# A two-block model kernel: products ordered by part, a token tile's last products by column halves, norm rows scaled on ScalarE

## Chip, core and metric

The kernel runs on one core of one Trainium2 chip. The metric is the device time of one execution in microseconds (us). TensorE (PE) does the matrix products, VectorE (DVE), ScalarE (ACT) and GpSimd (POOL) the work on elements, and SyncE (SP) issues most transfers.

## What is computed

The input is `x`, 256 tokens of 1024 values, all in float32. Two blocks follow each other. Cut to what matters here:

```
for layer in range(2):                                  # block 1
    qkv = rms_norm(x, g_mix[layer]) @ w_in[layer]
    mix = concat(differential(qkv), moba(qkv), dilated(qkv))
    x   = x + mix @ w_out[layer]                        # 1024 x 1024
    h2  = rms_norm(x, g_ffn[layer])
    x   = x + conv_gated_mlp(h2, w_up, conv_w, conv_b, w_down)
x = rms_norm(x, g_final)
h = rms_norm(x, norm1_g)                                # block 2
x = x + gates(ssm(h), sparse_attention(h)) @ w_out_2
h = rms_norm(x, norm2_g)
x = x + peer(h)      # top-16 routing, then gelu(h @ u.T) weighted @ v, 16384 experts
return rms_norm(x)

def rms_norm(x, g): return x * rsqrt(mean(x * x) + 1e-6) * g
```

## The kernel before

**Products.** Each float32 product is made of three products of reduced-precision parts: high by high, low by high, high by low, summed in the same PSUM bank. `mm3` (lines 149 to 153) issues the three for one slice of the contraction: line 151 is high by high, lines 152 and 153 each hold one low part. Which of the two low parts is that of the weights depends on the side on which the weights enter: in the trace's rows the moving operand stands first, then the stationary one.

**Weights.** `Weights` (L64) streams weight tiles of 128x1024 through SBUF in the order in which they are used. SP issues the load into one of four `raw` buffers; ACT copies it to the high part `whi` (L92); DVE subtracts to make the low part `wlo` (L94), or POOL does, for the tiles that `share` gives it. The parts have six buffers each, three in the last stage. `take`/`next` hand out tiles and split those that come after; `more(n)` splits until n tiles past the used ones are ready; `post` and `flush` hold back the evacuation of a PSUM bank to a chosen place in the order. All engines' orders are fixed when the program is built, by the order of these calls.

**The stages.** The matrix products of each stage follow each other on PE without a break in the program: the input projections, the attentions with their small products between weight tiles, the output projection, the up- and down-projections of the gated MLP (`layer_ffn`, with `up_mm` making 24 products of 256 columns for one weight tile), block 2's projections, the routing's queries and scores, 128 tiles of `u` (`u_pair`, L1691, two tiles of 24 products of 256 columns), and 128 tiles of `v` (`v_mm`, L1785, 12 products of 512 columns).

**The seam at a norm.** An output projection ends in `token_tiles` (L606): its last four weight tiles are all split by then, and are used for token tile 0 (the first 128 tokens), both column halves per weight tile, and then for token tile 1, in an order of (weight tile, half) steps of three products. `residual` (L657) adds a finished half to `x` on DVE. `rest` calls what the next norm has armed as `after_residual`. Three of the norms are armed by `arm_norm` (L665): that ahead of the gated MLP in each layer, and that ahead of the routing. There `after` multiplies by the gain on POOL (L675), squares and sums on ACT (L181), and, once a token tile's two halves are summed, finds the root on DVE (`rstd` L188, `rsqrt` L155: a first guess from the bits and three Newton steps on 128x1 values, lines 165 and 170) and scales the two halves of the row tile on DVE (L680). `ready` then calls `norm_T` (L197): eight transposes on PE (L204), the high part on ACT (L208), the low part on DVE (L209). `norm_at` says ahead of which step of token tile 1 token tile 0's transposes stand; `pool_splits` and `head_share` say which weight tiles POOL splits there. `head` (L637) makes the products with the next projection's first four weight tiles, token tile 0 first; ahead of its fourth weight tile stand the transposes of token tile 1. `arm_roots` (L693) and `arm_double` (L1885) are the other two kinds of norm; they scale later.

## Time and profile before

| | us |
|---|---|
| median of 3 runs | 1763.09 |
| the runs | 1757.03, 1763.09, 1763.2 |
| the profiled execution | 1756.17 |
| its span | 1754.2 |

The profile is of one execution of its own; its span is the time from the first to the last recorded instruction, and the 2 us between span and time lie around it. The granted clock of TensorE is 0.983 of full speed on average over the span. A stretch at "1.00" runs at 2.4 GHz, one at "0.50" at 1.2 GHz.

### The profile page before, as it was taken

The numbers are of one execution on the slowest core, as the hardware profiler recorded it, in microseconds if no ns is written. First come the engines' busy times: TensorE is split into PE (matmuls) and PEld (weight loads), VectorE is DVE, ScalarE is ACT, GpSimd is POOL, SyncE is SP. The second block draws the span as 40 slices with busy tenths as digits, with TensorE's granted clock in tenths as the row PEclk, the third lists the DMA queues.
The fourth block names the chain that finished last, engine by engine and source line by source line (L and its number), as shares of the span: only waits on it lengthen the run. The fifth ranks groups of instructions, "written<-read, shape, count | busy, mean of one in ns | idle before, by whom it ended". The sixth has DMA issues, their size and how long they took to land.

```text
span 1754.2 us, 29812 instructions
## 1 busy us (share of the span) xinstructions
PE 1675.0 (95%) x11558; PEld 1472.5 (84%) x11558; DVE 1262.0 (72%) x2260; ACT 842.2 (48%) x1286; POOL 603.0 (34%) x534
## 2 busy tenths in 40 slices
PE   8997999899979999989989989999999999999998
PEld 6786888787869898767869989999999888887776
DVE  6776898767767776696753998667777889864444
ACT  6554554655535555643434535543343444444444
POOL 3203438432038843681020444100000232345554
PEclk9998999999989999989999999999999999999999
DMA  7433455653334567723435445554454555555554
GB/s 253 143 120 121 144 176 168 216 186 132 121 132 158 170 200 251 285 84 104 156 123 180 156 164 186 181 173 165 157 164 162 167 170 169 168 180 191 187 187 155
DMA packets 84717, 294.09 MB, mean 168 GB/s; under 512 B 10800, under 2 KB 14928, under 8 KB 83680
## 3 DMA queue, kind: packets, MB, share of 16 engines
q1 hardware_dynamic: 83184, 286.19, 49.7%
q0 software_dynamic: 960, 5.47, 0.8%
q8 instruction: 91, 1.49, 0.3%
q10 hardware_dynamic: 432, 0.53, 0.1%
q14 instruction: 50, 0.41, 0.1%
HBM read 284.42 MB, written 7.34 MB: 166 GB/s over the span
## 4 chain that ended last, share of the span: by engine, by line
PE 74%; DVE 12%; POOL 5%; ACT 3%; issue 3%; DMA 2%; POOLq 0%; ACTq 0%; DVEq 0%; SPq 0%
PE acc L151 14%; PE acc L152 13%; PE acc L153 13%; PE side L151 8%; PE side L152 8%; PE side L153 8%; DVE wlo L94 3%; PE side L1686 3%; DVE cv L760 2%; ACT whi L92 2%; DVE rs_t L165 1%; POOL th L768 1%; PE side L385 1%; DVE rs_y L170 1%; PE side L204 1%
## 5 line engine op out<-in xcount | busy, mean ns | idle before, releaser
L94 DVE TENSOR_TENSOR wlo<-raw,whi 128x1024 fp32r<-128x1024 f32 x472 | 619.4, 1322 | 327.8 <-ACT whi L92 325.1
L92 ACT ACTIVATE whi<-raw 128x1024 fp32r<-128x1024 f32 x511 | 532.7, 1056 | 501.2 <-PE acc L152 231.2
L152 PE MATMUL side<-hTh,wlo 128*128 128x256 f32 x1664 | 471.4, 283 | 16.2 <-DVE wlo L94 14.8
L151 PE MATMUL side<-hTh,whi 128*128 128x256 f32 x1664 | 472.3, 284 | 0.2
L153 PE MATMUL side<-hTl,whi 128*128 128x256 f32 x1664 | 469.7, 282 | 0.0
L152 PEld LDWEIGHTS side<-hTh,wlo 128*128 128x128 f32 x1664 | 317.6, 191 | 20.5 <-DVE wlo L94 17.7
L151 PEld LDWEIGHTS side<-hTh,whi 128*128 128x128 f32 x1664 | 317.6, 191 | 2.6 <-ACT whi L92 0.7
L153 PEld LDWEIGHTS side<-hTl,whi 128*128 128x128 f32 x1664 | 317.8, 191 | 0.0
L1774 POOL TENSOR_TENSOR al<-S,ah 128x256 fp32r<-128x256 f32 x125 | 154.1, 1233 | 465.2 <-ACT ah L1773 465.2
L152 PE MATMUL acc<-whi,al 128*128 128x512 f32 x496 | 196.4, 396 | 0.0
L151 PE MATMUL acc<-whi,ah 128*128 128x512 f32 x496 | 195.1, 393 | 0.0
L153 PE MATMUL acc<-wlo,ah 128*128 128x512 f32 x496 | 193.2, 390 | 0.0
L151 PE MATMUL acc<-whi,hTh 128*128 128x512 f32 x384 | 161.7, 421 | 1.3 <-ACT whi L92 1.3
L152 PE MATMUL acc<-whi,hTl 128*128 128x512 f32 x384 | 154.9, 403 | 0.3 <-DVE hTl L209 0.3
L153 PE MATMUL acc<-wlo,hTh 128*128 128x512 f32 x384 | 154.6, 403 | 0.1
L94 POOL TENSOR_TENSOR wlo<-raw,whi 128x1024 fp32r<-128x1024 f32 x39 | 94.8, 2435 | 132.0 <-ACT whi L92 125.2
L152 PEld LDWEIGHTS acc<-whi,al 128*128 128x128 f32 x496 | 93.1, 188 | 28.7 <-POOL al L1774 7.5
L768 POOL TENSOR_TENSOR th<-th,cv 128x256 f32<-128x256 f32 x44 | 58.3, 1328 | 158.2 <-DVE th L767 121.0
L151 PEld LDWEIGHTS acc<-whi,ah 128*128 128x128 f32 x496 | 93.1, 188 | 19.5
L153 PEld LDWEIGHTS acc<-wlo,ah 128*128 128x128 f32 x496 | 93.2, 188 | 17.8
L760 DVE SCALAR_TENSOR_TENSOR cv<-side,cw,cv 128x254 f32<-128x254 f32 (+1 forms) x176 | 72.6, 474 | 30.9 <-ACT cv L757 30.9
L151 PEld LDWEIGHTS acc<-whi,hTh 128*128 128x128 f32 x384 | 74.8, 195 | 23.5 <-issue 6.5
(460 smaller groups left out, 2583.1 us busy)
## 6 DMA issues: line engine op xcount, KB each, us to landing
raw<-in_ws SPq DMA_DIRECT2D x259, 512.0 KB, 3.6
raw<-in_us SPq DMA_DIRECT2D x128, 512.0 KB, 3.4
raw<-in_vs SPq DMA_DIRECT2D x128, 512.0 KB, 3.3
dBst<-Bst SPq DMA_DIRECT2D x1, 2048.0 KB, 7.3
dCT<-CT SPq DMA_DIRECT2D x2, 1024.0 KB, 8.4
tg<-dBst POOLq DMA_DIRECT2D x1, 2048.0 KB, 10.3
gb<-in_g_ffn SPq DMA_DIRECT2D x2, 512.0 KB, 4.6
s5bc<-in_s5bc SPq DMA_DIRECT2D x2, 512.0 KB, 5.3
```

Of the source, the lines that this page charges most:

```text
L92: self.nc.scalar.activation(hi, t, AF.Copy)
L94: eng.tensor_tensor(lo, t, hi.bitcast(FT), op=OP.subtract)
L151: mm(ps, sh, mh, start=first, stop=False)
L152: mm(ps, sl, mh, start=False, stop=False)
L153: mm(ps, sh, ml, start=False, stop=last)
L165: V.scalar_tensor_tensor(t, y, h, y, op0=OP.mult, op1=OP.mult)
L170: V.scalar_tensor_tensor(o, t, 1.5, y, op0=OP.add, op1=OP.mult)
L204: nc.tensor.transpose(ps[:, 128 * i:128 * i + 128], src[:, c:c + 128], self.ident)
L760: nc.vector.scalar_tensor_tensor(o[which][:, n:], p[which][:, :S - n], cw[which][:, 2 - n:3 - n], o[which][:, n:], op0=OP.mult, op1=OP.add)
L768: nc.gpsimd.tensor_tensor(th, th, o[1], op=OP.mult)
L1686: nc.tensor.matmul(o, e2[:, n], e1[:, n, x], start=x == 0, stop=x == 2)
L1774: G.tensor_tensor(al, src, ah.bitcast(FT), op=OP.subtract)
```

## The change

Four things are edited. **(1)** `mm3` takes a list of products and issues all their high-by-high parts first, then all of one low side, then all of the other; `late` says which side's low part comes last ("s" the stationary one, "m" the moving one). With `mm_cols` a weight tile of an up-projection, of `u` or of the queries is eight products by `whi` with the high part, eight by `whi` with the low part, eight by `wlo`. **(2)** `rsqrt` of one column uses TENSOR_SCALAR with pointer scalars in place of SCALAR_TENSOR_TENSOR. **(3)** `token_tiles` does token tile 0's last two weight tiles by column halves, so that half 0 is finished one step of three products sooner. **(4)** `arm_norm` scales rows on ACT, in `ready`, right ahead of the transposes; these stand one step later; POOL splits other tiles and `hold` makes the splits there start later.

```diff
-    def mm3(self, ps, sh, sl, mh, ml, first, last):
+    def mm3(self, todo, late):
         mm = self.nc.tensor.matmul
-        mm(ps, sh, mh, start=first, stop=False)
-        mm(ps, sl, mh, start=False, stop=False)
-        mm(ps, sh, ml, start=False, stop=last)
+        for ps, sh, sl, mh, ml, first, last in todo:
+            mm(ps, sh, mh, start=first, stop=False)
+        for side in "ms" if late == "s" else "sm":
+            for ps, sh, sl, mh, ml, first, last in todo:
+                mm(ps, sl if side == "s" else sh, ml if side == "m" else mh, start=False, stop=last and side == late)
+
+    def mm_cols(self, ps, wt, T, n=128):
+        cs = [(k, slice(128 * k, 128 * k + n)) for k in range(8)]
+        self.mm3([(ps, wt[0][:, c], wt[1][:, c], T[0][:, k], T[1][:, k], k == 0, k == 7) for k, c in cs], "s")
...
             if n == 1:
-                V.scalar_tensor_tensor(t, y, h, y, op0=OP.mult, op1=OP.mult)
+                V.tensor_scalar(t, y, y, h, op0=OP.mult, op1=OP.mult)
+                V.tensor_scalar(o, t, 1.5, y, op0=OP.add, op1=OP.mult)
...
         wts = w.take(4, 2)
-        for i in range(4):
-            if i:
+        for i, h in ((0, 0), (0, 1), (1, 0), (1, 1), (2, 0), (3, 0), (2, 1), (3, 1)):
+            if i and not h:
                 w.flush()
-            mms(0, i, wts[i], (0, 1))
-            if hook:
+            mms(0, i, wts[i], (h,))
+            if h and hook:
                 hook(i)
-        for h in range(2):
-            self.residual(0, h, ps[0][h])
-            self.rest(0, h)
+            if (i, h) == (3, 0):
+                self.residual(0, 0, ps[0][0])
+                self.rest(0, 0)
+        self.residual(0, 1, ps[0][1])
+        self.rest(0, 1)
...
-                w.more(min(3 + i, 4))
+                w.more(min(3 + max(i - self.hold, 0), 4))
...
             if h:
-                r = self.rstd(ms[:, t])
-                for x in (xn[t][:, 512 * i:512 * i + 512] for i in range(2)):
-                    self.nc.vector.tensor_scalar(x, x, r, None, op0=OP.mult)
+                root[t] = self.rstd(ms[:, t])
 
         def ready(t):
-            self.norm_T(xn.pop(t), hT, t)
+            x = xn.pop(t)
+            for h in range(2):
+                v = x[:, 512 * h:512 * h + 512]
+                self.nc.scalar.activation(v, v, AF.Identity, scale=root[t])
+            self.norm_T(x, hT, t)
 
-        self.norm_at, self.residual_at, self.pool_splits, self.head_share = (2, 1), (3, 0), (0, 1), 1
+        self.norm_at, self.residual_at, self.pool_splits, self.head_share = (3, 1), (3, 0), (0, 3), 1
+        self.hold = 2
...
         def up_mm(ps, which, wt):
-            for k in range(8):
-                c = slice(128 * k, 128 * k + 128)
-                self.mm3(ps[:, 256 * which:256 * which + 256], wt[0][:, c], wt[1][:, c], hh[:, k], hl[:, k], k == 0, k == 7)
+            self.mm_cols(ps[:, 256 * which:256 * which + 256], wt, hT)
...
-        def v_mm(c, A, wt, t, h):
-            tk = slice(128 * t, 128 * t + 128)
-            cc = slice(512 * h, 512 * h + 512)
-            self.mm3(acc[t][h], A[0][:, tk], A[1][:, tk], wt[0][:, cc], wt[1][:, cc], c == 0, c == 127)
+        def v_mm(c, A, wt, th):
+            self.mm3([(acc[t][h], *(x[:, 128 * t:128 * t + 128] for x in A), *(x[:, 512 * h:512 * h + 512] for x in wt),
+                       c == 0, c == 127) for t, h in th], "s")
```

The other callers of `mm3` get lists in the same way, with "m" (the moving weights' low part last) in the input and output projections and "s" in `head`. `arm_roots` and `arm_double` set `hold = 0`.

ScalarE at the first `arm_norm` norm, that ahead of the gated MLP of layer 0, from the attention's last evacuations (`mixTh`) to the high parts of the second token tile (`hTh`; `ms` takes the sum of squares, `rs_y` is the root), before:

```order
L448 ACTIVATE mixTh<-side 128x256 x4
L181 ACTIVATE squares,ms<-x 128x512 x2
L92 ACTIVATE whi<-raw 128x1024 x2
L208 ACTIVATE hTh<-side 128x4x128 x2
L181 ACTIVATE squares,ms<-x 128x512 x2
L92 ACTIVATE whi<-raw 128x1024 x2
L208 ACTIVATE hTh<-side 128x4x128 x2
L92 ACTIVATE whi<-raw 128x1024 x3
```

and of the change:

```order
L459 ACTIVATE mixTh<-side 128x256 x4
L192 ACTIVATE squares,ms<-x 128x512 x2
L92 ACTIVATE whi<-raw 128x1024
L192 ACTIVATE squares,ms<-x 128x512
L699 ACTIVATE xn<-xn,rs_y 128x512 x2
L219 ACTIVATE hTh<-side 128x4x128 x2
L92 ACTIVATE whi<-raw 128x1024
L192 ACTIVATE squares,ms<-x 128x512
L92 ACTIVATE whi<-raw 128x1024 x2
L699 ACTIVATE xn<-xn,rs_y 128x512 x2
L219 ACTIVATE hTh<-side 128x4x128 x2
L92 ACTIVATE whi<-raw 128x1024 x3
```

The squares of token tile 1's first half come ahead of the first `hTh`, two row scalings stand ahead of each `hTh` pair, and the two weight copies that stood between the first squares and the first `hTh` are spread out. On DVE the two scalings L680 are gone at each place, and the root's six steps stand at the same place in another form.

GpSimd at the same norm (`gb` is the gain, `xn` the row tile, `th` belongs to the gated MLP after it), before:

```order
L675 TENSOR_TENSOR xn<-x,gb 128x512 x2
L94 TENSOR_TENSOR wlo<-raw,whi 128x1024 x2
L768 TENSOR_TENSOR th<-th,cv_1686 128x256
L768 TENSOR_TENSOR th<-th,cv_1696 128x256
L768 TENSOR_TENSOR th<-th,cv_1745 128x256
```

and of the change:

```order
L690 TENSOR_TENSOR xn<-x,gb 128x512
L94 TENSOR_TENSOR wlo<-raw,whi 128x1024
L690 TENSOR_TENSOR xn<-x,gb 128x512
L94 TENSOR_TENSOR wlo<-raw,whi 128x1024 x2
L784 TENSOR_TENSOR th<-th,cv_1686 128x256
L784 TENSOR_TENSOR th<-th,cv_1696 128x256
L784 TENSOR_TENSOR th<-th,cv_1745 128x256
```

The two splits of each pair are drawn apart: one stands between the row tile's halves of token tile 1, and two after them.

PE at the end of the layer-0 `head` and the first weight tiles of the up-projection (`side` is the bank of an up-projection, `hTh` and `hTl` the two parts of the normed rows), before, where the three products of each slice alternate:

```order
L151 MATMUL acc<-whi,hTh 128x512
L152 MATMUL acc<-whi,hTl 128x512
L153 MATMUL acc<-wlo,hTh 128x512
L151 MATMUL side<-hTh,whi 128x256
L152 MATMUL side<-hTh,wlo 128x256
L153 MATMUL side<-hTl,whi 128x256
L151 MATMUL side<-hTh,whi 128x256
```

and of the change:

```order
L154 MATMUL acc<-whi,hTh 128x512 x2
L157 MATMUL acc<-wlo,hTh 128x512 x2
L157 MATMUL acc<-whi,hTl 128x512 x2
L154 MATMUL side<-hTh,whi 128x256 x8
L157 MATMUL side<-hTl,whi 128x256 x8
L157 MATMUL side<-hTh,wlo 128x256 x8
```

The first product with `wlo` of a weight tile was its second of 24, and is now its seventeenth; the last product with `whi` was its 24th, and is now its sixteenth.

## Rows read from the trace of the kernel before

**Rows 1.** The page: the span, and the busy time of each engine.

```profile
span 1754.2 us, 29812 instructions
...
PE 1675.0 (95%) x11558; PEld 1472.5 (84%) x11558; DVE 1262.0 (72%) x2260; ACT 842.2 (48%) x1286; POOL 603.0 (34%) x534
```

**Rows 2.** Waits of PE: us in total, times, longest wait in us.

```profile
PE side L204 <- DVE xn L680: 23.7, 5, 5.7
PE side L152 <- DVE wlo L94: 14.8, 13, 1.8
...
PE acc L152 <- DVE wlo L94: 4.8, 1, 4.8
```

**Rows 3.** Timeline of PE in two stages: start, length, what it does.

```profile
999.78 0.28 PE L153 MATMUL side<-hTl,whi 128*128 128x256 f32 x1
999.90 0.28 PE L151 MATMUL side<-hTh,whi 128*128 128x256 f32 x1
...
1499.71 0.39 PE L153 MATMUL acc<-wlo,ah 128*128 128x512 f32 x1
1499.94 0.39 PE L151 MATMUL acc<-whi,ah 128*128 128x512 f32 x1
```

**Rows 4.** Timeline around the first gated-MLP norm of layer 0.

```profile
130.83 1.39 DVE L659 TENSOR_TENSOR x<-acc,x 128x512 f32<-128x512 f32 x2 [2.54 <-PE acc L153]
...
131.10 0.40 PE L153 MATMUL acc<-wlo,mixTh 128*128 128x512 f32 x1
...
131.60 2.57 POOL L675 TENSOR_TENSOR xn<-x,gb 128x512 f32<-128x512 f32 x2 [17.48 <-DVE x L659]
...
133.35 0.21 DVE L191 TENSOR_SCALAR var<-ms 128x1 f32<-128x1 f32 x1 [1.13 <-ACT squares L181]
...
133.60 0.15 DVE L161 TENSOR_SCALAR rs_y<-var 128x1 int32<-128x1 int32 x1
...
134.54 4.67 POOL L94 TENSOR_TENSOR wlo<-raw,whi 128x1024 fp32r<-128x1024 f32 x2 [0.37 <-ACT whi L92]
...
134.67 2.25 DVE L170 SCALAR_TENSOR_TENSOR rs_y<-rs_t,rs_y 128x1 f32<-128x1 f32 x1
...
139.87 0.88 DVE L680 TENSOR_SCALAR xn<-xn,rs_y 128x512 f32<-128x512 f32 x2 [0.46 <-DVE rs_y L170]
...
140.51 1.94 PE L204 MATMUL side<-ident,xn 128*128 128x128 f32 x8 [4.81 <-DVE xn L680]
...
141.63 0.60 ACT L208 ACTIVATE hTh<-side 128x512 fp32r<-128x512 f32 x1 [5.77 <-PE side L204]
```

**Rows 5.** Windows: stretch, length, PE, PEld, DVE, ACT, POOL busy, granted clock.

```profile
137.80:144.60 6.80, 4.09 (x14) 3.64 (x15) 4.45 (x7) 1.80 (x4) 2.69 (x2) 0.50 0.44 155
...
sum 34.20, PE 23.74 PEld 20.65 DVE 20.16 ACT 8.23 POOL 9.40; mean PE 4.75 PEld 4.13 DVE 4.03 ACT 1.65 POOL 1.88
```

**Rows 6.** Groups of ScalarE by line and form: count, busy, mean ns.

```profile
L92 ACT ACTIVATE whi<-raw 128x1024 fp32r<-128x1024 f32 x511 | 532.7, 1056 | 501.2 <-PE acc L152 231.2 <-PE side L153 221.8 <-PE acc L153 22.0
...
L181 ACT ACTIVATE squares<-x 128x512 f32<-128x512 f32 x28 | 17.6, 630 | 30.7 <-DVE x L659 28.8 <-POOL x L1914 1.1 <-ACT squares L181 0.3
...
L1829 ACT ACTIVATE hTh<-raw,rs_y 128x512 f32<-128x512 f32 x2 | 1.4, 723 | 3.9 <-DVE rs_y L170 3.9
```

**Rows 7.** Windows: the up-projections of layer 0, and the routing.

```profile
192.00:275.00 83.00, 76.69 (x525) 69.47 (x524) 73.21 (x179) 45.66 (x69) 35.51 (x30) 1.00 0.51 165
1000.00:1032.00 32.00, 25.44 (x206) 24.62 (x204) 31.96 (x118) 11.89 (x14) 16.68 (x7) 1.00 0.37 132
```

**Rows 8.** Timeline at 221 us: GpSimd and VectorE at once.

```profile
221.13 2.39 POOL L94 TENSOR_TENSOR wlo<-raw,whi 128x1024 fp32r<-128x1024 f32 x1
...
221.24 2.32 DVE L841 TENSOR_SCALAR ex_n<-ex_n 128x16 f32<-128x16 f32 x1
```

**Rows 9.** Timeline at 1005 us, in the routing: the same pair.

```profile
1005.55 2.38 POOL L94 TENSOR_TENSOR wlo<-raw,whi 128x1024 fp32r<-128x1024 f32 x1 [2.11 <-ACT whi L92]
...
1005.77 3.25 DVE L94 TENSOR_TENSOR wlo<-raw,whi 128x1024 fp32r<-128x1024 f32 x1
```

More of the change, by code (lines that the diff above doesn't have):

```diff
@@ L168, in rsqrt @@
                 V.tensor_tensor(t, t, h, op=OP.mult)
-            o = y if out is None or i < iters - 1 else out
-            V.scalar_tensor_tensor(o, t, 1.5, y, op0=OP.add, op1=OP.mult)
+                V.scalar_tensor_tensor(o, t, 1.5, y, op0=OP.add, op1=OP.mult)
         return o
@@ L593, in mms @@
             tk = slice(128 * t, 128 * t + 128)
-            for h in hs:
-                c = slice(512 * h, 512 * h + 512)
-                self.mm3(ps[t][h], T[0][:, k, tk], T[1][:, k, tk], wt[0][:, c], wt[1][:, c], first, last)
+            cs = [(h, slice(512 * h, 512 * h + 512)) for h in hs]
+            self.mm3([(ps[t][h], T[0][:, k, tk], T[1][:, k, tk], wt[0][:, c], wt[1][:, c], first, last) for h, c in cs], "m")
         for i, k in enumerate(ks[:4]):
@@ L668, in arm_norm @@
         hT = self.new_T(self.hTp, "hT")
-        xn = {}
+        xn, root = {}, {}
         ms = self.xnp.tile([128, 2, 2], FT, name="ms")
@@ L1334, in wide @@
             tk = slice(128 * t, 128 * t + 128)
-            for h in hs:
-                c = slice(512 * h, 512 * h + 512)
-                self.mm3(ps[t][h], T[0][:, k, tk], T[1][:, k, tk], wt[0][:, c], wt[1][:, c], first, last)
+            cs = [(h, slice(512 * h, 512 * h + 512)) for h in hs]
+            self.mm3([(ps[t][h], T[0][:, k, tk], T[1][:, k, tk], wt[0][:, c], wt[1][:, c], first, last) for h, c in cs], "m")
         def ev_attn(t, ps):
@@ L1414, in block2 @@
             if b == 1:
-                wh, wl = w.next()
-                for k in range(8):
-                    c = slice(128 * k, 128 * k + 40)
-                    self.mm3(ps[0][0:40, 0:S], wh[:, c], wl[:, c], hh[:, k], hl[:, k], k == 0, k == 7)
+                self.mm_cols(ps[0][0:40, 0:S], w.next(), hT, 40)
                 late["small"] = z[0:40, 0].rearrange("p g r -> p (g r)")[:, 0:S]
@@ L1444, in block2 @@
             wh, wl = w.next()
+            nT = late["nT"]
             for t in range(2):
-                for kk in range(2):
-                    k = 2 * i + kk
-                    tk = slice(128 * t, 128 * t + 128)
-                    c = slice(512 * kk, 512 * kk + 512)
-                    nT = late["nT"]
-                    self.mm3(ps[t], nT[0][:, k, tk], nT[1][:, k, tk], wh[:, c], wl[:, c], k == 0, k == 3)
+                tk = slice(128 * t, 128 * t + 128)
+                cs = [(2 * i + kk, slice(512 * kk, 512 * kk + 512)) for kk in range(2)]
+                self.mm3([(ps[t], nT[0][:, k, tk], nT[1][:, k, tk], wh[:, c], wl[:, c], k == 0, k == 3) for k, c in cs], "m")
             run(m)
@@ L1518, in peer @@
         w.limit = len(w.tiles)
-        hh, hl = hT
         sp = P("peer", 1)
@@ L1568, in q_mm @@
             for hf in range(2):
-                wh, wl = w.next()
-                for k in range(8):
-                    c = slice(128 * k, 128 * k + 128)
-                    self.mm3(ps[:, 256 * hf:256 * hf + 256], wh[:, c], wl[:, c], hh[:, k], hl[:, k], k == 0, k == 7)
+                self.mm_cols(ps[:, 256 * hf:256 * hf + 256], w.next(), hT)
             return ps
@@ L1693, in u_pair @@
             for x in range(2):
-                wh, wl = w.next()
+                wt = w.next()
                 if x and between:
                     between()
-                for k in range(8):
-                    cc = slice(128 * k, 128 * k + 128)
-                    self.mm3(ps[:, 256 * x:256 * x + 256], wh[:, cc], wl[:, cc], hh[:, k], hl[:, k], k == 0, k == 7)
+                self.mm_cols(ps[:, 256 * x:256 * x + 256], wt, hT)
             if c == 64:
@@ L1797, in peer @@
             nxt = a_split(c + 1)
-            for t in range(2):
-                for h in range(2):
-                    v_mm(c, A, wt, t, h)
+            v_mm(c, A, wt, [(t, h) for t in range(2) for h in range(2)])
             if c % 2 == (c > 30):
```

34 lines of the change are left out of this document (18 added, 16 removed).

## The prediction

> **What bounds it now.** I read the page first: PE is busy for 1675.0 us of 1754.2, 95% [rows 1], so the products are the bound and what can be saved is mostly the 79 us in which PE stands still, and the time in which it runs at half its clock. The waits of PE came next, as they say what the standing still is for. Of those that this change can touch the largest is that of the transposes on the scaled rows at three norms: five waits, 23.7 us in all. Then come the low parts of weights: 13 waits of products with 256 columns, 14.8 us, none over 1.8, and one single wait of 4.8 us [rows 2]. The other long waits lie in the attentions, the state space part and the load at the start, where the change has only its order of products.
>
> The windows give the clock's share. There are five stretches at 0.50 to 0.51 of full clock (1.2 GHz for 2.4), one right behind each of those five norm waits. Together they last 34.20 us, with PE busy for 23.74 of them [rows 5]. At full clock that work would take half, so the half clock costs 11.9 us. The norm waits thus cost 23.7 + 11.9 = 35.6 us in all; that is the largest piece.
>
> The timeline at one norm shows why they are so long [rows 4]. DVE makes the sum of squares ready at 133.35, but scales only at 139.87. Between lie steps on 128x1 values. One that ran while POOL split weights (134.54, 4.67 us for two) took 2.25 us, and the two scalings came behind. POOL's splits, on no path of their own, thus held up PE.
>
> **Scaling and transposes, first token tile.** Times are those of the layer-0 norm. A product of 512 columns starts 0.23 us after the one before [rows 3], so a step of three is 0.70. Token tile 0's last product starts at 131.10 and token tile 1 begins at 131.33 [rows 4]. Before, PE reached the transposes after six steps, at 135.5, and began them at 140.51. Now there are seven: 136.2.
>
> The root: the second half's residual ends at 130.83 + 1.39 = 132.2, as before, and the first DVE step can start at 133.35 or a little sooner. The first two steps are 0.25 apart [rows 4]; at this pace nine steps end at 133.35 + 9 x 0.25 = 135.6.
>
> It is not the root that is late next but ACT, whose order has token tile 1's first squares ahead of the scaling. That half is finished after six steps, 131.33 + 4.2 + 0.2 = 135.7; its residual takes 0.70 (half of 1.39), its square 0.63 [rows 6] and about 0.2 to read out, so 137.2. For a scaling I take the one of the same shape that ACT already does, 0.72 [rows 6]: the first is done at 137.95. PE waits 137.95 - 136.2 = 1.8 us, and about 0.4 more between the fourth and the fifth transpose, as these take less time than the second scaling. Three norms: 3 x 2.2 = 6.6.
>
> **Second token tile.** The first transposes end near 139.0. PE then has three projection products and 18 of `head`: 21 x 0.233 = 4.9, so 143.9. The high parts (0.60 each [rows 4]) are ready at 139.6, the low parts on DVE, of about 0.7 each, at 140.4, and only then comes the last half's residual: 141.1. Square to 141.9; nine DVE steps to 144.4. Two weight copies of 1.06 [rows 6] stand ahead of the scaling on ACT: 144.0, hidden by the root. POOL's split there (2.34, half of 4.67) and its half row tile (1.29, half of 2.57) end near 144.3 [rows 4], hidden too. First scaling to 145.1: a wait of 1.2 and 0.3 inside the transposes, 1.5. In two layers that is 3.0. At the norm of block 2 the second token tile has no wait now; for the same chain without the copies ahead of it I take 1.2.
>
> Sum of the norm waits after: 6.6 + 3.0 + 1.2 = 10.8, so 12.9 us less. That the half clock goes with them is a choice: no row shows a wait of 2 us with its clock behind it. The stretches here stand behind waits of 4 us and more; waits of up to 1.8 us [rows 2] have none in the window of the routing, whose clock is 1.00 [rows 7]. 2.2 is nearer to the second, so I take all 11.9. **Norms: 24.8**, with bounds of 12.9 (every stretch comes back) and 30 (the waits of the second tiles and half of the rest go as well).
>
> **Low parts later.** In a weight tile of 24 products `wlo` is needed after 16 and not after one. At 0.12 us [rows 3] that is 15 x 0.12 = 1.8 us later, and the longest of the 13 waits is 1.8 [rows 2]: taken alone, each would go. Four of the 13 lie in the routing, one for each 7.7 us, 7.2 us in all; the rest, 7.6, in the gated MLPs.
>
> What keeps me from taking all of it is DVE. In the up-projections of layer 0 it is busy for 73.21 of 83.00 us and PE for 76.69; in the routing for 31.96 of 32.00, PE for 25.44 [rows 7]. If DVE is the bound, delaying a need only moves the wait. In the gated MLP there is room, since PE alone would need more than DVE's 73.2: 5 of 7.6, bounds 2 and 7.6. In the routing PE's idle 6.6 us are mostly that one wait, and its cause is a collision: DVE's split took 3.25 us as POOL's split (2.38) began 0.22 before it, and ended 1.1 after that one's end [rows 9]; alone it would be about that 1.1. With `whi` free eight products sooner POOL's split starts about 1 us sooner, so part of the collision goes. I take 4, bounds 1.8 (one wait in four) and 7.2. The single wait of 4.8 us stands behind the second of 24 products with `wlo`: 1.8 less, up to 3.5 with the half clock after it.
>
> The new order itself I cost at nothing: as many products, as many weight loads. Rows where the operand alternates and where the slice or the bank changes are 0.12 apart with 256 columns, and 0.23 apart with 512 [rows 3]. Column halves at the end of token tile 0 move a residual 0.70 sooner that nothing waited for: 0.
>
> **A rule against it.** The step of 2.25 us has two inputs from SBUF and ran beside POOL's split; the new form has one and scalars. In this trace such steps of 128x1 took 0.21 and 0.15 at 133.35 and 133.60, inside POOL's 2.57 from 131.60 [rows 4], so I cost them as free of POOL. But one of 128x16 took 2.32 beside a split of 2.39 [rows 8]. The Trainium skill, SBUF — State Buffer, section "Who interferes with whom", says that an instruction with two SBUF inputs contends with GpSimd's reads, and that tensor_scalar can enter a two-port mode and then contends too. By that rule the root might be held up as before; the 128x16 row agrees with it, the 128x1 rows don't. The sum by it would be rival A's 1733.
>
> **Sum.** 24.8 + 5 + 4 + 1.8 = 35.6. The profiled execution took 1756.2, so 1720.6. The runs shown lie 0.9 to 7 us above it, the median 6.9; I add 2, between the lowest and the median, for **1722**. By the bounds: 12.9 + 2 + 1.8 + 1.8 = 18.5 and 30 + 7.6 + 7.2 + 3.5 = 48.3, so 1708 to 1745 with 0.9 to 7 added.
>
> **Rivals.** *A, the root stays blocked.* Every 128x1 step started beside POOL waits for it: at the second token tile the split, 2.34, then the row tile, of which 0.3 delays it, so 2.6, and a part of a half-clock stretch, 1.7 of the 2.4 that one costs (11.9 / 5); at the first 0.7. Two layers: 2 x (2.6 + 1.7), three first tiles 3 x 0.7, in sum 10.7, so 1733. For it: the 128x16 row. Against: the 128x1 rows.
>
> *B, the low parts' waits only move.* DVE or POOL are the bound in those stages, and neither the 5 nor the 4 comes: 1731. For it: 31.96 of 32.00. Against: the long split there is a collision of two [rows 9], and in the gated MLP DVE has 9.8 us of 83 free [rows 7].
>
> *C, slower: the order of products costs.* If a product following one with the same weights' part or into another bank started later by a few ns, all 11,558 would pay. It decides from 35.6 / 11,558 = 3.1 ns; at 6 ns it is 69 us for a gain of 36, so 1791. Rows 3 show to 10 ns that changes of bank and operand cost nothing, which is much against it; nothing shows the new sequence itself.
>
> *D, nothing moves.* ACT's scaling is as late as DVE's was, since the squares ahead of it wait in turn. It needs 3 us more on each of five waits, with the clock back: 1722 + 15 + 12 + 9 = 1758. No row speaks for 3 us more.
>
> **Numbers.** Forecast 0.60; A 0.12; B 0.16; C 0.07; D 0.05. What a measurement here can tell from no change is about 0.5%, 9 us. Forecast, A and B are faster: 0.88. D is the same, and C slower with a mishap not thought of. The range holds forecast, A and B with their bounds: 1702 to 1745, the low end 6 below the bounds' sum since the end of waits in the other stages was costed at nothing.
>
> **What would show it.** The waits of the transposes: on ACT's scaling, about 2 us and 1.5, six of them. The step after the guess on DVE under 0.3 us beside POOL; over 2 means A. The windows behind the norms at 1.00. Products 0.12 and 0.23 apart as now; otherwise C. In the routing, `wlo` waits gone and DVE's split near 1.3 us; if PE still idles 6 us of 32 there, B. The prediction is wrong if waits for ACT take more than 4 us at a norm, or if PE's waits on `whi` grow where those on `wlo` went.

## The result: 2.5% faster, and where the time came from

The changed kernel took 1716.7 us (median of 4 runs, 1715.53 to 1717.6), the kernel before 1761.91 in runs beside it: a ratio of 0.9748, 95% interval 0.9727 to 0.9769. 1722 had been forecast. Its profiled execution has a span of 1713.6 us, 40.6 less than before.

The page of the changed kernel, its span and the busy time of each engine, to be read against [rows 1]:

```profile
span 1713.6 us, 29782 instructions
...
PE 1660.6 (97%) x11558; PEld 1468.0 (86%) x11558; DVE 1243.8 (73%) x2248; ACT 850.6 (50%) x1298; POOL 623.3 (36%) x534
```

PE's idle time went from 79.2 us to 53.0. Its busy time fell by 14.4 us with as many products, mostly since a product at half clock counts for as long as it runs; 26.2 and 14.4 make the 40.6. The waits of PE in the changed kernel, us in total, times and longest, against [rows 2]:

```profile
PE side L215 <- ACT xn L699: 7.3, 6, 1.5
...
PE side L154 <- ACT whi L92: 5.8, 5, 1.8
...
PE acc L157 <- DVE wlo L94: 3.3, 3, 2.6
...
PE side L157 <- DVE wlo L94: 1.0, 1, 1.0
```

The transposes wait 7.3 us where they waited 23.7, and now for ScalarE's scaling. The waits of products with 256 columns on `wlo` from DVE went from 14.8 to 1.0. New are 5.8 us in which such products wait for `whi`. The timeline of the changed kernel around the first of the three norms (its clock is 0.7 us behind there, from a later start):

```profile
134.54 0.27 DVE L176 TENSOR_SCALAR rs_t<-rs_y,rs_h 128x1 f32<-128x1 f32 x1
...
135.22 2.39 POOL L94 TENSOR_TENSOR wlo<-raw,whi 128x1024 fp32r<-128x1024 f32 x1 [0.93 <-ACT whi L92]
...
135.97 0.21 DVE L177 TENSOR_SCALAR rs_y<-rs_t,rs_y 128x1 f32<-128x1 f32 x1
...
136.42 0.69 DVE L674 TENSOR_TENSOR x<-acc,x 128x512 f32<-128x512 f32 x1 [0.24 <-PE acc L157]
...
137.21 0.63 ACT L192 ACTIVATE squares<-x 128x512 f32<-128x512 f32 x1 [2.06 <-DVE x L674]
...
137.84 1.32 ACT L699 ACTIVATE xn<-xn,rs_y 128x512 f32<-128x512 f32 x2
...
138.60 1.27 PE L215 MATMUL side<-ident,xn 128*128 128x128 f32 x8 [1.51 <-ACT xn L699]
...
144.91 1.34 ACT L699 ACTIVATE xn<-xn,rs_y 128x512 f32<-128x512 f32 x2 [0.37 <-DVE rs_y L177]
...
145.69 1.27 PE L215 MATMUL side<-ident,xn 128*128 128x128 f32 x8 [0.91 <-ACT xn L699]
```

Against [rows 4]: the root's steps L176 and L177 take 0.21 to 0.28 us each, the last ones beside POOL's split of 2.39 from 135.22, where one took 2.25. The root is ready at 136.2, DVE takes the next residual, and the scaling starts behind the squares of token tile 1's first half. PE waits 1.5 us, and at the second token tile 0.9. All five half-clock stretches of [rows 5] are gone. One is new: behind the longest wait for `whi`, 1.8 us, the window 282.60 to 286.00 us has a granted clock of 0.52, so 1.2 GHz for nearly all of it.

Two windows of the changed kernel, the up-projections of layer 0 (4 us earlier than in [rows 7]) and the routing; columns are the length, busy time of PE, PEld, DVE, ACT and POOL, granted clock and DMA:

```profile
188.00:271.00 83.00, 78.61 (x542) 71.65 (x542) 73.40 (x176) 44.61 (x68) 38.91 (x33) 1.00 0.53 170
1000.00:1032.00 32.00, 32.00 (x269) 32.00 (x269) 31.39 (x104) 16.90 (x20) 15.89 (x6) 1.00 0.61 202
```

PE fills the routing window, where it had 25.44 of 32. In the gated MLP it gained little: 78.61 for 76.69, with DVE as busy as before.

Both traces hold 11,558 products of PE, so the start of the n-th in one can be set against the n-th in the other. The difference, taken at the borders of stages, gives the account:

```
stage                                   us gained   forecast
start and attention, layer 0               -0.7        0
norm, layer 0                              10.4     } 
norm, layer 1, and the tiles behind it     11.5     } 24.8
norm ahead of the routing                   3.6     }
gated MLP, layer 0                          0.1     } 5
gated MLP, layer 1, to block 2              1.4     }
block 2 to its norm                         0.3        0
query tile                                  2.2        1.8
routing                                     6.7        4
other u tiles and the gate transposes       1.1        0
v tiles beside the gate transposes          0.0        0
last v tiles                                4.4        0
sum                                        41.0       35.6
```

### The profile page after: what moved, and what is told of

It is laid out like the page before. It is cut to its first block, busy times and chain, and to the rows that moved or that the text cites. A ratio compares the mean times of both kernels' runs of the same rounds, so it can differ in the third digit from the quotient of the medians.

```text
span 1713.6 us, 29782 instructions
## 1 busy us (share of the span) xinstructions
PE 1660.6 (97%) x11558; PEld 1468.0 (86%) x11558; DVE 1243.8 (73%) x2248; ACT 850.6 (50%) x1298; POOL 623.3 (36%) x534
## 3 DMA queue, kind: packets, MB, share of 16 engines
q8 instruction: 90, 1.47, 0.3%
## 4 chain that ended last, share of the span: by engine, by line
PE 76%; DVE 12%; ACT 3%; POOL 3%; issue 3%; DMA 2%; ACTq 0%; DVEq 0%; POOLq 0%
PE acc L157 27%; PE side L157 17%; PE acc L154 14%; PE side L154 9%; DVE wlo L94 4%; PE side L1690 3%; DVE cv L776 1%; ACT whi L92 1%; DMA raw<-in_ws 1%; PE side L396 1%; POOL BB L967 1%; PE side L373 1%; DMA Kst<-dKst 1%; PE side L372 1%; DVE S L1508 1%
## 5 line engine op out<-in xcount | busy, mean ns | idle before, releaser
L154 PE MATMUL side<-hTh,whi 128*128 128x256 f32 x1664 | 235.5, 284 | 5.9 <-ACT whi L92 5.8
L157 PE MATMUL side<-hTh,wlo 128*128 128x256 f32 x1664 | 232.8, 282 | 1.0 <-DVE wlo L94 1.0
L157 PE MATMUL side<-hTl,whi 128*128 128x256 f32 x1664 | 233.0, 283 | 0.0
L154 PEld LDWEIGHTS side<-hTh,whi 128*128 128x128 f32 x1664 | 215.1, 191 | 10.3 <-ACT whi L92 7.2
L157 PEld LDWEIGHTS side<-hTh,wlo 128*128 128x128 f32 x1664 | 213.5, 191 | 1.4 <-DVE wlo L94 1.2
L157 PEld LDWEIGHTS side<-hTl,whi 128*128 128x128 f32 x1664 | 214.0, 191 | 0.0
L154 PE MATMUL acc<-whi,ah 128*128 128x512 f32 x496 | 134.2, 392 | 0.0
L157 PE MATMUL acc<-wlo,ah 128*128 128x512 f32 x496 | 132.7, 389 | 0.0
L157 PE MATMUL acc<-whi,al 128*128 128x512 f32 x496 | 132.7, 389 | 0.0
L157 PEld LDWEIGHTS acc<-wlo,hTh 128*128 128x128 f32 x384 | 72.9, 190 | 19.5 <-DVE wlo L94 1.8
```

Source lines behind the costliest of these rows:

```text
L154: mm(ps, sh, mh, start=first, stop=False)
L157: mm(ps, sl if side == "s" else sh, ml if side == "m" else mh, start=False, stop=last and side == late)
```

## The experiments

Each kernel was timed beside the kernel before, not all on one occasion, so they stand against each other by their ratios to it; 0.001 is 1.76 us. The changed kernel's is 0.9748. A difference of two ratios is uncertain by some 0.003, 5 us. "By the trace" is the difference of spans of single profiled executions. Such spans also differ, by 1 to 3 us in a stage, where no edit reaches: in some of these executions PE has a half-clock stretch near 285, 305 or 775 us, in others not.

| kernel | ratio to before | 95% interval | span, us |
|---|---|---|---|
| the change | 0.9748 | 0.9727 to 0.9769 | 1713.6 |
| old order of products | 0.9862 | 0.9845 to 0.9878 | 1731.9 |
| old form of the root's steps | 0.9894 | 0.9878 to 0.9911 | 1739.2 |
| scaling on DVE | 0.9808 | 0.9792 to 0.9825 | 1720.6 |
| old places at the norm | 0.9748 | 0.9731 to 0.9764 | 1711.9 |
| old order of halves | 0.9760 | 0.9746 to 0.9775 | 1712.8 |
| before, new form of the root's steps | 0.9961 | 0.9941 to 0.9980 | 1745.2 |
| before, new order of products | 0.9897 | 0.9878 to 0.9916 | 1740.9 |
| the change, scaling ahead of squares | 0.9787 | 0.9768 to 0.9807 | 1719.7 |
| the change, v tiles in two lists | 0.9770 | 0.9755 to 0.9785 | 1715.9 |
| the change, tanh later | 0.9675 | 0.9656 to 0.9694 | 1703.2 |
| the change, tanh later, old places | 0.9664 | 0.9651 to 0.9677 | 1695.6 |
| the same, and the conversion later | 0.9638 | 0.9625 to 0.9651 | 1696.9 |

**The order of products, undone.**

```diff
         for ps, sh, sl, mh, ml, first, last in todo:
             mm(ps, sh, mh, start=first, stop=False)
-        for side in "ms" if late == "s" else "sm":
-            for ps, sh, sl, mh, ml, first, last in todo:
-                mm(ps, sl if side == "s" else sh, ml if side == "m" else mh, start=False, stop=last and side == late)
+            mm(ps, sl, mh, start=False, stop=False)
+            mm(ps, sh, ml, start=False, stop=last)
```

> The changed kernel with the three products of each slice alternating again, all else as changed. Theory (the order of products gave what the norms did not: routing 6.7 us, the v stage's last part 4.4, the gated MLP of layer 1 about 2.3, the query tile about 2): about 15 us slower than the changed kernel, so near 1732, with PE's 6.6 idle us back in the routing window and the norm waits as changed. Rival (the order counts only where the two splits collide, in the routing, and at the query tile): 8 to 9 us slower, so near 1725.

It is slower than the changed kernel by 0.0114, 20 us, and by 18.3 by the trace: the theory's side, and 3 to 5 us more than its 15. Its waits of PE:

```profile
PE side L155 <- DVE wlo L94: 13.7, 12, 1.8
PE side L214 <- ACT xn L698: 6.9, 6, 1.5
```

The 12 waits on `wlo` are back, with the norm waits still short. Set product against product, 8.1 us are lost in the routing, 4.1 in the last v tiles, 1 in the gated MLP of layer 1, about 2 at the query tile, 1 in the other u tiles; some 2 fall in block 2, where a half-clock stretch came that the changed kernel's profile doesn't have.

**The form of the root's steps, undone.**

```diff
-                V.tensor_scalar(t, y, y, h, op0=OP.mult, op1=OP.mult)
-                V.tensor_scalar(o, t, 1.5, y, op0=OP.add, op1=OP.mult)
+                V.scalar_tensor_tensor(t, y, h, y, op0=OP.mult, op1=OP.mult)
+                V.scalar_tensor_tensor(o, t, 1.5, y, op0=OP.add, op1=OP.mult)
```

> The changed kernel with the root's six steps as SCALAR_TENSOR_TENSOR again. Theory (these steps wait for POOL's splits, TENSOR_SCALAR of 128x1 doesn't): the first token tile's root 2 us later, which holds up the residual and squares that stand ahead of the scaling on ScalarE, 1.9 us at three norms; the second token tile's 3 to 5 us at two or three; half clock behind the longer waits: 10 to 28 us slower than the changed kernel, near 1737. Rival (only the places of the splits mattered, not the form of the step): under 3 us slower.

0.0146 slower, 26 us, and 25.6 by the trace. With the other parts in place the two lines are thus worth more than half of the change. The timeline of this kernel at the first norm:

```profile
136.28 2.38 POOL L94 TENSOR_TENSOR wlo<-raw,whi 128x1024 fp32r<-128x1024 f32 x1 [0.93 <-ACT whi L92]
136.30 2.38 DVE L177 SCALAR_TENSOR_TENSOR rs_y<-rs_t,rs_y 128x1 f32<-128x1 f32 x1
...
139.04 0.68 DVE L674 TENSOR_TENSOR x<-acc,x 128x512 f32<-128x512 f32 x1
...
140.45 1.32 ACT L699 ACTIVATE xn<-xn,rs_y 128x512 f32<-128x512 f32 x2
...
141.21 1.97 PE L215 MATMUL side<-ident,xn 128*128 128x128 f32 x8 [3.07 <-ACT xn L699]
...
148.45 4.66 POOL L94 TENSOR_TENSOR wlo<-raw,whi 128x1024 fp32r<-128x1024 f32 x2
...
148.55 2.29 DVE L176 SCALAR_TENSOR_TENSOR rs_t<-rs_y,rs_h 128x1 f32<-128x1 f32 x1
...
150.87 2.26 DVE L177 SCALAR_TENSOR_TENSOR rs_y<-rs_t,rs_y 128x1 f32<-128x1 f32 x1
...
154.45 1.97 PE L215 MATMUL side<-ident,xn 128*128 128x128 f32 x8 [4.56 <-ACT xn L699]
```

One step is held by a split of 2.38, and with it the residual, the squares and the scaling behind it, so PE waits 3.1 us; at the second token tile two steps are held for 2.3 us each, and PE waits 4.6. The clock falls behind it, in a window over the stretch after the first of these waits:

```profile
140.20:147.00 6.80, 5.79 (x18) 4.92 (x19) 2.93 (x7) 5.43 (x11) 3.06 (x2) 0.50 0.16 64
```

**The scaling on DVE again.**

```diff
-                root[t] = self.rstd(ms[:, t])
+                r = self.rstd(ms[:, t])
+                for x in (xn[t][:, 512 * i:512 * i + 512] for i in range(2)):
+                    self.nc.vector.tensor_scalar(x, x, r, None, op0=OP.mult)
...
-            x = xn.pop(t)
-            for h in range(2):
-                v = x[:, 512 * h:512 * h + 512]
-                self.nc.scalar.activation(v, v, AF.Identity, scale=root[t])
-            self.norm_T(x, hT, t)
+            self.norm_T(xn.pop(t), hT, t)
```

> The changed kernel with the two row scalings on VectorE again, right behind the root. Theory (a TENSOR_SCALAR of 128x512 with all operands in SBUF waits for POOL's splits, the 128x1 steps don't): the first token tiles 0.5 us sooner or the same, the second ones 2.4 to 4.7 us later, as POOL's pair of splits begins just when the root is ready; 4 to 13 us slower than the changed kernel, near 1725. Rival (once the root is quick, it doesn't matter which engine scales): within 3 us of it.

0.0060 slower, 10.5 us (7.0 by the trace). The two scalings, 0.88 us before where POOL was idle [rows 4], stand in this kernel's timeline at the second token tile so:

```profile
145.70 0.21 DVE L177 TENSOR_SCALAR rs_y<-rs_t,rs_y 128x1 f32<-128x1 f32 x1
146.03 2.97 DVE L695 TENSOR_SCALAR xn<-xn,rs_y 128x512 f32<-128x512 f32 x2
146.15 5.09 POOL L94 TENSOR_TENSOR wlo<-raw,whi 128x1024 fp32r<-128x1024 f32 x2
...
146.66 0.63 PE L215 MATMUL side<-ident,xn 128*128 128x128 f32 x4 [1.12 <-DVE xn L695]
...
149.14 0.63 PE L215 MATMUL side<-ident,xn 128*128 128x128 f32 x4 [1.86 <-DVE xn L695]
```

They take 2.97 us, and PE does four transposes, waits 1.86 and does the other four. A 128x512 step of the same operation as the 128x1 ones waits for POOL's split; the 128x1 ones don't. At first token tiles the wait was a little shorter than with ScalarE (0.95), as expected.

**The places of before.**

```diff
-        self.norm_at, self.residual_at, self.pool_splits, self.head_share = (3, 1), (3, 0), (0, 3), 1
-        self.hold = 2
+        self.norm_at, self.residual_at, self.pool_splits, self.head_share = (2, 1), (3, 0), (0, 1), 1
+        self.hold = 0
```

> The changed kernel with the places of before: transposes one step sooner, POOL's splits at steps 0 and 1, no hold. Theory (with the scaling on ScalarE and the quick root, where POOL's splits stand no longer counts): PE's wait for the scaled rows 0.7 us longer at each first token tile but the same work behind it; within 3 us of the changed kernel. Rival (the places are what keeps POOL out of the way): 5 us slower or more, with longer root steps.

The same ratio, 0.9748. Its norm waits are shorter, not 0.7 us longer at the first token tiles as expected. The waits of PE:

```profile
PE side L215 <- ACT xn L699: 3.6, 6, 0.8
```

The scaling stands ahead of the squares of token tile 1's first half there, as the transposes do, so these no longer hold it up. Product against product the three norms are 1.2 us each quicker than in the changed kernel, too little for the ratio to tell. With the scaling on ScalarE this part of the change brought nothing.

**The order of column halves, undone.**

```diff
-        for i, h in ((0, 0), (0, 1), (1, 0), (1, 1), (2, 0), (3, 0), (2, 1), (3, 1)):
+        for i, h in ((0, 0), (0, 1), (1, 0), (1, 1), (2, 0), (2, 1), (3, 0), (3, 1)):
```

> The changed kernel with token tile 0's last two weight tiles in the old order, both halves of one and then both of the other. Theory (half 0's residual comes 0.7 us later, but the root waits for half 1, and ScalarE for token tile 1's first half): no change, within 2 us of the changed kernel. Rival (the two halves' residuals and squares then come close together and hold up the root): 3 us slower or more, with the root's first step later at every norm.

0.9760, with the changed kernel's 0.9748 inside its interval, and 0.8 us less by the trace, with the same 7.3 us of norm waits: no change, as costed.

**One part on the kernel before: the root's steps.** The two lines of the second experiment, the other way round, in the kernel before.

```diff
             if n == 1:
-                V.scalar_tensor_tensor(t, y, h, y, op0=OP.mult, op1=OP.mult)
+                V.tensor_scalar(t, y, y, h, op0=OP.mult, op1=OP.mult)
...
-            V.scalar_tensor_tensor(o, t, 1.5, y, op0=OP.add, op1=OP.mult)
+            if n == 1:
+                V.tensor_scalar(o, t, 1.5, y, op0=OP.add, op1=OP.mult)
```

> The kernel before with one part of the change: the root's six steps as TENSOR_SCALAR. Theory (a root is no longer held up by POOL's splits, but the scaling of 128x512 on VectorE behind it is, so both halves are needed for the gain): the root ready 3.5 us sooner, the scalings each behind a split of POOL, the transposes finished under 1 us sooner; 4 to 10 us faster than before, part of it from the half clock. Rival (the form of the root's steps is the whole gain at the norms): some 20 us faster than before.

0.0039 faster, 7 us (3.5 to 10); its runs spread from 1747.15 to 1756.59, and the profiled one is the fastest, so the 9.0 by the trace is on the high side. The timeline of this kernel at the first norm:

```profile
134.55 4.86 POOL L94 TENSOR_TENSOR wlo<-raw,whi 128x1024 fp32r<-128x1024 f32 x2 [0.37 <-ACT whi L92]
...
135.29 0.21 DVE L171 TENSOR_SCALAR rs_y<-rs_t,rs_y 128x1 f32<-128x1 f32 x1
...
135.96 3.73 DVE L683 TENSOR_SCALAR xn<-xn,rs_y 128x512 f32<-128x512 f32 x2 [0.46 <-DVE rs_y L171]
...
137.35 0.63 PE L207 MATMUL side<-ident,xn 128*128 128x128 f32 x4 [1.64 <-DVE xn L683]
...
139.83 1.09 PE L207 MATMUL side<-ident,xn 128*128 128x128 f32 x4 [1.86 <-DVE xn L683]
```

The root is ready at 135.5 and not at 139.4. But the two scalings behind it now take 3.73 us for 0.88, and PE waits twice, 1.64 and 1.86. The transposes end 1.5 us sooner than before (140.92 for 142.45), where under 1 was expected. Taking one obstacle away let the next one be met.

**One part on the kernel before: the order of products.** The edit of `mm3`; its callers get their lists as in the change.

```diff
-        mm(ps, sh, mh, start=first, stop=False)
-        mm(ps, sl, mh, start=False, stop=False)
-        mm(ps, sh, ml, start=False, stop=last)
+        for ps, sh, sl, mh, ml, first, last in todo:
+            mm(ps, sh, mh, start=first, stop=False)
+        for side in "ms" if late == "s" else "sm":
+            for ps, sh, sl, mh, ml, first, last in todo:
+                mm(ps, sl if side == "s" else sh, ml if side == "m" else mh, start=False, stop=last and side == late)
```

> The kernel before with the new order of products alone (norms, root and token halves as before). Theory (the order's gain, 18.3 us between the traces of the changed kernel and of the one with the old order, stands by itself, since it lies in other stages than the norms): 15 to 20 us faster than before, PE without idle time in the routing window, the norm waits 23.7 us as before. Rival (the gains depend on each other: splits that come sooner or later at the norms set the pace behind them): under 12 us faster, or over 23.

0.0103 faster, 18 us (15 to 21; 13.3 by the trace), with 23.5 us of norm waits. The order stands by itself. The parts at the norm do not: 18 of the order and 7 of the root's steps make 25 of the change's 44. The other 19 come only where the quick steps meet other parts: all the rest without them (0.9894) is worth no more than the order alone (0.9897). With the scaling back on DVE (0.9808) 34 us of gain stay, 9 more than the 25, so some 9 come with the new places and halves and without ScalarE; the scaling on ScalarE gives the last 10, and with it the places no longer matter. These two shares are uncertain by 5 us or so, and no run has the quick steps with the new places alone, or with ScalarE's scaling alone.

**The scaling ahead of everything.**

```diff
-                root[t] = self.rstd(ms[:, t])
+                r = self.rstd(ms[:, t])
+                for v in (xn[t][:, 512 * i:512 * i + 512] for i in range(2)):
+                    self.nc.scalar.activation(v, v, AF.Identity, scale=r)
...
-            x = xn.pop(t)
-            for h in range(2):
-                v = x[:, 512 * h:512 * h + 512]
-                self.nc.scalar.activation(v, v, AF.Identity, scale=root[t])
-            self.norm_T(x, hT, t)
+            self.norm_T(xn.pop(t), hT, t)
```

> The changed kernel with the row scalings on ScalarE right behind the root, ahead of the weight copies and of the squares of token tile 1's first half. Theory (at the first token tile the scaling waits 1.5 us for those squares and not for the root): 1 us less wait at three first token tiles, 2 to 4 us faster than the changed kernel. Rival (ScalarE then stands still for the root with two weight copies behind it, and PE waits for these instead): no faster, waits on whi or hTh up by what the scaling gave.

0.0039 slower, 7 us: the theory failed and the rival held in kind. The waits of PE in this kernel:

```profile
PE side L215 <- ACT xn L695: 5.6, 6, 1.3
...
PE acc L154 <- ACT hTh L219: 2.7, 5, 0.7
PE acc L154 <- ACT whi L92: 2.4, 2, 1.3
```

The transposes wait 1.7 us less, but products wait 2.7 us for `hTh`, which now stands behind a weight copy and the squares and was no wait in the changed kernel; a half-clock stretch of 3.4 us more stands at the last of the three norms. Product against product the norms lose 1.0, 0.7 and 1.7 us; the other 2.7 of the 6.1 by the trace lie in stages that the edit doesn't touch. ScalarE's queue has one order, and what is moved up moves the rest down.

**Why the gated MLP gained nothing.**

```diff
-            th = fp.tile([128, S], FT, name="th", bufs=4)
-            nc.scalar.activation(th, o[0], AF.Tanh, scale=0.5)
-            w.post(gated, j, th, o)
+            w.post(gated, j, o)
 
-        def gated(j, th, o):
+        def gated(j, o):
+            th = fp.tile([128, S], FT, name="th", bufs=4)
+            nc.scalar.activation(th, o[0], AF.Tanh, scale=0.5)
```

> The changed kernel with the gated MLP's tanh issued one evacuation later on ScalarE, behind the next weight copies and not ahead of them. It asks why the order of products brought nothing in layer 0's gated MLP, where PE now waits 5.8 us for whi. Theory 1 (the weight copy stands on ScalarE behind a tanh that waits for VectorE's convolution steps): these waits go, 3 to 6 us faster than the changed kernel. Theory 2 (VectorE is the bound there, 73 of 83 us busy, and the wait only shows on another engine): the same time within 2 us, with waits on wlo or on the gated rows in place of those on whi.

0.0073 faster than the changed kernel, 13 us (10.4 by the trace; product against product about 10 in layer 0 and 2 in layer 1, with 2 lost in stages that the edit doesn't touch): theory 1, and more than it expected. PE's waits for `whi` in both gated MLPs are gone. The changed kernel's timeline ahead of PE's longest wait for `whi`, 1.8 us that end near 282.2, shows the queue:

```profile
278.48 1.00 ACT L773 ACTIVATE cv<-side,cw 128x256 f32<-128x256 f32 x2
...
279.52 1.65 DVE L776 SCALAR_TENSOR_TENSOR cv<-side,cw,cv 128x255 f32<-128x255 f32 x4 [2.81 <-ACT cv L773]
280.87 0.42 ACT L779 ACTIVATE th<-cv 128x256 f32<-128x256 f32 x1 [1.39 <-DVE cv L776]
...
281.19 2.94 ACT L92 ACTIVATE whi<-raw 128x1024 fp32r<-128x1024 f32 x3
```

ScalarE stands idle 1.39 us ahead of the tanh `th`, until DVE has finished its four convolution steps `cv`, and three weight copies stand behind it. PE waits for the first, and the new half-clock stretch follows. In the kernel with the tanh later, the place of the same weight tiles:

```profile
269.24 1.01 ACT L773 ACTIVATE cv<-side,cw 128x256 f32<-128x256 f32 x2
...
270.14 1.06 ACT L92 ACTIVATE whi<-raw 128x1024 fp32r<-128x1024 f32 x1
...
270.28 1.65 DVE L776 SCALAR_TENSOR_TENSOR cv<-side,cw,cv 128x255 f32<-128x255 f32 x4 [4.29 <-ACT cv L773]
...
271.64 0.42 ACT L782 ACTIVATE th<-cv 128x256 f32<-128x256 f32 x1 [0.44 <-DVE cv L776]
...
271.96 2.00 ACT L92 ACTIVATE whi<-raw 128x1024 fp32r<-128x1024 f32 x2
```

A weight copy goes ahead of the tanh, beside DVE's steps. In its window PE is busy without a break, with DVE at 76.48 of 83:

```profile
188.00:271.00 83.00, 83.00 (x588) 77.67 (x587) 76.48 (x173) 46.97 (x71) 44.84 (x41) 1.00 0.61 189
```

In the window from 183 to 266 us DVE is at 80.59 of 83, with PE as busy. So DVE kept up, if with little room, and theory 2 falls.

**The last v tiles.**

```diff
-            v_mm(c, A, wt, [(t, h) for t in range(2) for h in range(2)])
+            for h in range(2):
+                v_mm(c, A, wt, [(t, h) for t in range(2)])
```

> The changed kernel with the 12 products of a v tile in two lists of six (one column half, both token tiles), not one of twelve. It asks what took 4.1 us out of the last v tiles, where before one product in 24 was followed 0.31 us and not 0.23 us later by the next. The waits for the three inputs stand at the first, second and third product before, at the first, fifth and ninth in the changed kernel, here at the first, third and fifth; a stationary part is used twice in a row only in the changed kernel. Theory 1 (the waits one right behind the other): as fast as the changed kernel, within 1 us in the v stage's trace. Theory 2 (the stationary part used twice in a row): 4 us slower there, as before.

0.9770, and 2.3 us more by the trace, but these lie ahead of the v tiles; the v tiles run as in the changed kernel, within 0.25 us. So it is not the stationary part used twice in a row. Nor is theory 1 the cause, though its number came out: the trace of the kernel before, read again for PE's weight loads in the last v tiles, shows what is. Their waits from 1540 to 1745 us, and the timeline of one case, in the kernel before:

```profile
PEld acc L152 <- POOL al L1774: 7.3, 31, 0.3
```

and, by start and length,

```profile
1649.80 1.47 POOL L1774 TENSOR_TENSOR al<-S,ah 128x256 fp32r<-128x256 f32 x1 [1.36 <-ACT ah L1773]
...
1651.33 0.19 PEld L152 LDWEIGHTS acc<-whi,al 128*128 128x128 f32 x1 [0.23 <-POOL al L1774]
1651.35 0.47 PE L152 MATMUL acc<-whi,al 128*128 128x512 f32 x1
...
1651.66 0.39 PE L153 MATMUL acc<-wlo,ah 128*128 128x512 f32 x1
```

The low part `al` of the gated values, made on POOL in 1.47 us, was the stationary part of a tile's second product, and just late. The load of it waited, 31 times and 7.3 us in all, and the product behind began 0.31 after it (1651.35 to 1651.66) and not 0.23. Summed over the last v tiles, the products right behind those by `al` are late by 3.4 us, most of the 4.4. With the old order in the changed kernel the loads wait again, 60 times and 11.8 us; in the changed kernel and in this one they don't. The new order needs `al` at the ninth product of a tile, the two lists at the fifth; both are late enough.

**Two versions that beat the change.** The tanh later and the places of before (the two diffs above together), and then also

```diff
-        V.tensor_copy(itb.rearrange("p a b -> p (a b)"), it)
+        w.post(V.tensor_copy, itb.rearrange("p a b -> p (a b)"), it)
```

> The changed kernel with the tanh one evacuation later and the places of before at the norms, both of which the runs so far spoke for. Theory (the two lie in different stages, 10.4 and 2 us by the traces): 12 us faster than the changed kernel, ratio to the kernel before near 0.967. Rival (they share the weight splits behind the norm): 8 us or less.

> The kernel of the run before this one in the same call (tanh later, old places) with the conversion of the index row, which waits on VectorE for a transfer, put behind the next evacuations and so behind three weight splits. Theory (the wait of 2.6 us at the query tile is that conversion's, with 1.7 us of half clock behind it): 2.6 to 4.3 us faster than without, and no wait on wlo at the query tile. Rival (the weights there are late themselves): no difference.

The first has 0.9664, 0.0084 or 15 us better than the change; the second 0.9638. Timed side by side, the medians are 1698.35 and 1694.35: 4.0 us, within what was expected. PE's waits on `wlo` ahead of a product with an `acc` bank, 3.1 us in the first, are 0.5 in the second, and product against product the query tile is 4.1 us quicker. That the second has the longer span, by 1.3 us, is no answer to this: its profiled execution was the slowest of its five, and what it lost lies near 305 and 760 us, where PE ran at half clock.

## Why the prediction held, step by step

**What bounds it** and **the norms**: right in mechanism and in the sum, 25.5 us for 24.8. The two terms of it are less close. The forecast took its own waits, counted from start to start, from a 23.7 that counts from the end of a product. Counted alike, the waits fell by 16.4 us (23.7 to 7.3) where 12.9 was forecast, which leaves 9.1 for the clock and all else there, where 11.9 was forecast. With the 0.7 us by which this trace lags there, the root was ready at 135.5 (135.6 forecast), the first transposes started at 137.9 (137.95), the second scaling at 144.2 (144.4). The wait was set by the squares ahead of the scaling on ScalarE, as argued; the old places, which took them from there, shortened it to 0.8. Six waits make 7.3 us where 10.8 was forecast, mostly because the forecast counted from start to start. That no half clock follows the waits that are left was a choice, and came out, but on waits of 1.5 us and not on the 2.2 that it was made for. Its reason, that no row shows a wait of 2 us with its clock behind it, overlooked one: in the trace of the kernel before PE waits 2.39 us near 310.8, and the window 311.80 to 315.40 has a clock of 0.53.

**The rule against it and rival A.** The 128x1 steps took 0.21 to 0.28 beside POOL's splits, so A didn't come. The kernel with the old form of the steps shows what A would have been: 26 us, where A was priced at 10.7. A had counted 0.7 us more wait at a first token tile, and there PE waits 2.65 to 3.07 us for 1.51; and it had counted part of one half-clock stretch in each layer, where two came.

The Trainium skill, SBUF — State Buffer, section "Who interferes with whom", says that a DVE instruction with two SBUF inputs contends with a GpSimd instruction that reads SBUF. The old form's 2.38 us beside a split agrees. The Trainium skill says in the same section that tensor_scalar can enter two-port modes, and then contends, when its operands meet conditions. The 128x512 pairs, 2.97 and 3.73 us, agree. The Trainium skill, VectorE: DVE Perf Modes, section "Mode 2×_2P", names as a condition that the outermost dimension larger than one be even, or odd and equal on both sides. That one element has no such dimension to split, and that the 128x1 steps go free for that reason, is a reading that the 0.21 to 0.28 us fit and that no run here tests.

D's late ScalarE came to 1.5 us and not to 5.

**Low parts later: the step that failed is "in the gated MLP there is room ... 5 of 7.6".** It brought 0.1 us in layer 0 and at most 1.4 in layer 1. (Of the 14.8 us, 6.9 lie in the routing and 8.0 in the gated MLPs; the prediction had 7.2 and 7.6, which changes little.) One of the two signs that the prediction named against itself came here: PE's waits on `whi` grew, to 5.8 us, where those on `wlo` went. The reason that the prediction gave against taking all, that DVE is the bound, was not it either: with the tanh moved, PE ran without a break beside DVE at 76 to 81 of 83 us. The wait moved to ScalarE's queue, where a tanh waiting for DVE held up weight copies. No row was read for what stands ahead of `whi` there. Rival B's result was thus right for this stage and its reason wrong. In the routing 4 was too little: all of PE's 6.6 us came back, as POOL's split began sooner and from 981.54 on no longer met DVE's, which began at 983.87 and took 1.20 us; before, they began at 1013.27 and 1013.62, and DVE's took 3.12. The query tile gave 2.2 for 1.8.

**The order costs nothing**: right as to a cost, so C didn't come: 269 products in the 32.00 us of the routing window are 0.12 us apart, as in [rows 3]. But the last v tiles, counted as 0, gave 4.4 us: the order also moves back the need for `al`, and the waits that this took away stand in the rows of the weight loads, which the prediction didn't read. That is as much as the gated MLPs missed (5 for 1.5). That 1717 came so near to 1722 owes something to these two cancelling, which is luck.

**Halves and places**: no gain, as costed for the halves; for the places the prediction had one step more of work ahead of the transposes as part of the gain, and the run without it is as fast, with waits of 0.8 us for 1.5.

## What to carry to other kernels

A step on VectorE of 128x1 that read two operands from SBUF took 2.25 to 2.38 us beside a GpSimd split of 2.38, as long as the split; rewritten with the second operand as a pointer scalar it took 0.21 to 0.28. Wide steps, 128x512, were held in that form too, and were better on ScalarE. When the first consumer of a late operand is moved back, look for what the next engine's queue holds ahead of the other operand, here a tanh that waited for VectorE ahead of three weight copies. Parts of a change at one seam are not added up: the root's steps alone gave 7 us, and their removal cost 26.

## What the runs showed of the hardware

- The same VectorE operation beside a GpSimd split: 128x1 takes 0.21 to 0.28 us, 128x16 2.32 [rows 8], two of 128x512 3.73 where they took 0.88 beside none.
- At the norms of the changed kernel, waits of PE of 1.5 us and 0.9 us left its clock at 2.4 GHz; norm waits of 2.65 us and more, in the kernels that had them, came with a stretch at 1.2 GHz. Between these the length alone didn't decide. In the kernel before with the new root's steps, waits of 1.64 and 1.86 us at the norm of layer 0 had a stretch (138.60 to 145.60, clock 0.51), and waits of 1.65 and 1.86 at that of layer 1 had none (485 to 502, clock 1.00).
- A wait of a weight load of up to 0.3 us shows on PE as a product that is followed 0.31 us later, and not 0.23, with no idle time: most of the 4.4 us of the last v tiles, which PE's own waits don't hold.
